# Sum steps fewer ahead of the first norm, low parts behind the copies of dilated keys, a head's four squares together

## The chip, the cores and the metric

The kernel runs on one core of a Trainium2 chip, in one launch. The time is the device time in microseconds (us). A core has five engines, each with an instruction stream of its own that it takes in order: TensorE (PE in the profile) multiplies matrices, VectorE (DVE), ScalarE (ACT) and GpSimd (POOL) work on tiles, and SyncE (SP) here only issues transfers. Engines wait for each other by semaphores. DMA transfers are put into queues by SP and POOL (in the profile SPq and POOLq are those engines' issuing) and are carried out by 16 DMA engines that all queues share.

## The reference

One layer of a decoder trunk, in float32, for 512 tokens of 1024 channels:

```python
proj = x @ w_in                               # 1024 -> 10752
o_da = diff_attention(...)                    # 4 heads: two softmax maps, w = p0 - lam * p1
                                              # o * rsqrt(mean(o^2) + eps) * norm_g, per head
o_sb = stick_breaking_attention(...)          # 8 heads
o_dl = dilated_attention(...)                 # 12 heads in 3 groups, dilations 1, 4, 16
merged = g0 * (o_da @ w_da) + g1 * (o_sb @ w_sb) + g2 * (o_dl @ w_dl)    # g = sigmoid(gates)
x = layer_norm(ALPHA * x + merged @ w_out)    # the first norm
c = square(relu(x @ w_up)) @ w_down           # 1024 -> 4096 -> 1024
ple = sigmoid(x @ w_ple_gate) * (p @ w_ple)
x = layer_norm(ALPHA * x + c + ple)
```

The inputs are x, p and the weights; the output is x. The first norm's result is the input of both the MLP and the gate of `ple`.

## The kernel before

**Products.** A float32 product is three PE matmuls on high and low parts (`mm3`, L86 to L89: high x high, low x high, high x low). Most of the large products are in a form with seven instead of eight block products, which needs sums of weight blocks. These sums are made in DRAM, by transfers from DRAM to DRAM on POOL's queue: a copy, then transfers that add to it. `vsum`, `qsum`, `msum`, `bsum`, `gsum`, `usum` and `dsum` are such sums, `usum` those for w_up and `dsum` those for w_down; names like `usum_3` in the order below are buffers of them. Each such transfer is a *sum step* (`sum_steps`; issued at L1247 when it adds, at L1249 when it copies), and it waits for a mark, the DVE subtraction that made the low part of a weight chunk some four chunks earlier.

**Weights.** A weight chunk (128x1024) is loaded by SP (L213, some by POOL at L176) into one of six raw buffers `raw`. ACT casts it to its high part `wh` (L262), DVE subtracts for the low part `wl` (L264), into a ring of five; PE reads both. A load into a raw buffer goes out when the subtraction has freed the buffer.

**The order.** The main loop goes through a list of *items*, each some matmuls with a bank of PSUM and an evacuation, and between them takes pieces of the heads' work (generators, `step`). Behind each item it adds to `credit`: the item's size times its `rate` up to the fifth item of the output product, nothing for a stretch, and 0.72 an item from the seventh behind the start of `ple`. Each whole credit issues one sum step. So `rate` says how many sum steps an item brings. From this program a scheduler makes each engine's order; `tc.high_priority()` lets an instruction come early in it, and `tc.issue_after(i)` puts what is inside behind instruction `i`.

**The three places.**

- *Dilated keys.* The projection's product for a dilated head's keys `dl_k` is computed into a PSUM bank and copied out by DVE at high priority (L346, in `t_evac`). `u4l` and `u5l` (L292) are low parts of sums of x that the seven-product form needs; their high parts `u4h` and `u5h` are cast on ACT (L291). `oT` (L1885) and `e`, `sph`, `spl`, `sml` (L1820 to L1857) are stick-breaking attention's.
- *Differential heads.* `da_block` handles one head and one block of 128 queries: logits, exponentials (L1916), transposes of the weights, the product with the values (L1944) into a quarter of a bank `po` that the head's four blocks share, and a square on ACT with its sum over the row (L1949, tile `scr`, sums in `ss`). After the fourth block come mean and root (L1954 to L1963, tile `ms`), the product of `po` with them (L1965, tile `on`), transposes on PE (L1971) and a copy to `oT`.
- *First norm.* `wout_items` computes merged @ w_out in eight items (four blocks of 128 tokens, two halves of 512 channels), each with rate 3.2 (L1055). Behind a block's second half `layer_norm_act` runs: sums of squares on ACT, two steps of the variance on DVE (L1001, L1002, tile `lr`), the power -1/2 on POOL (L1003), then the scaled rows `xn` on DVE (L1005, L1013). PE transposes `xn` (L1078), ACT casts it to `x1hT` (L1084) and DVE makes the low part `x1lT` (L1085); ACT makes `x1r` (L1091). The product `p @ w_ple` (L1109 to L1111) lies beside this; the gate product (L1169 to L1171) reads the norm's result, and the up products come after it, copied out by ACT (L1358, tile `up`).

Of the kernel before, what the change touches and what calls it, by code (L numbers as in the profile page):

```python
# [10 lines left out]
F32 = mybir.dt.float32  # L11
F32R = mybir.dt.float32r
BF16 = mybir.dt.bfloat16
AF = mybir.ActivationFunctionType
# [4 lines left out]
P = 128  # L19
# [36 lines left out]
def trunk(tc, a, out):  # L56
    nc = tc.nc
    es = ExitStack()
    with es:
        big = es.enter_context(tc.tile_pool(name="big", bufs=64))  # L60
        ring = es.enter_context(tc.tile_pool(name="ring", bufs=1))
        one = es.enter_context(tc.tile_pool(name="one", bufs=1))
# [7 lines left out]
        def nm(s):  # L70
            uid[0] += 1
            return f"{s}_{uid[0]}"

        def slot(name, dt=F32):
            return big.tile([P, 512], dt, name=nm(name), tag="s", bufs=NSLOT)
# [79 lines left out]
        st = {"dma": 0, "split": 0, "ring": 0}  # L155
# [12 lines left out]
        def chunk(src, w):  # L168
            return chunk_of(load(src, w))
# [68 lines left out]
        def split_next():  # L238
            c = chunks[st["split"]]
            w, off = c["w"], c.get("off", 0)  # L240
            if c.get("pre"):
                c["pre"]()
            st["ring"] += not c.get("aside")
            if c.get("apart"):
                hs, ls = [[slot(n, F32R) for _ in range(2)] for n in ("wh", "wl")]
                parts = [(hs[i], ls[i], 512 * i, 512 * i + 512) for i in range(2)]
                c["h"], c["l"] = Halves(hs), Halves(ls)
            elif c.get("beside"):
                h, lo = c["beside"]["tiles"]
                parts = [(h[:, 512:512 + w], lo[:, 512:512 + w], 0, w)]  # L250
                c["h"], c["l"] = parts[0][:2]
            elif c.get("dst") is None:
                h = ring.tile([P, 1024], F32R, name=nm("wh"), tag="wh", bufs=RING)
                lo = ring.tile([P, 1024], F32R, name=nm("wl"), tag="wl", bufs=RING)
                parts = [(h[:, :w], lo[:, :w], 0, w)]
                c["h"], c["l"] = parts[0][:2]
                c["tiles"] = h, lo
            else:
                parts = c["dst"]
            for h, lo, a0, a1 in parts:  # L260
                raw = c["from"]["raw"][:, off + a0:off + a1]
                i = nc.scalar.copy(h, raw)  # L262
                st["cast"] = getattr(i, "ins", i)
                i = nc.vector.tensor_sub(lo, raw, h.bitcast(F32))  # L264
                st["low"] = getattr(i, "ins", i)
                lows.append(st["low"])
                marks.append(st["low"])
            for t in (c["from"], *c.get("also", ())):
                t["uses"] -= 1
            if c.get("then"):  # L270
                c["then"]()
            st["split"] += 1
# [11 lines left out]
        items = []  # L284
# [24 lines left out]
        scale = {"da_q": 0.125, "sb_q": 0.125, "dl_q": 128.0 ** -0.5}  # L309
# [18 lines left out]
        def t_evac(name, j):  # L328
            def ev(ps):
                sc = scale.get(name, 1.0)  # L330
                if name in ("sb_k", "da_q"):
                    T[name, j] = evac_stacked(ps, name, sc)
                elif name in ("sb_q", "da_k"):
                    T[name, j] = evac_twice(ps, name, sc)
                else:
                    t = slot(name)
                    if j < 4:
                        o, i = t, ps
                    else:
                        o = t.rearrange("p (c n) -> p c n", c=4)  # L340
                        i = ps.rearrange("p (n c) -> p c n", c=4)
                    if name == "dl_q":
                        nc.scalar.activation(o, i, AF.Copy, scale=sc)
                    else:
                        with tc.high_priority():
                            nc.vector.tensor_copy(o, i)  # L346
                    T[name, j] = t
            return ev

# [678 lines left out]
        def wout_items():  # L1028
            for half in range(2):
                cs = [chunk(a["wo"][half, c].rearrange("p k n -> p (k n)"), 1024) for c in range(4)]  # L1030
                for tt in range(4):
                    ks = (4, 5, 6, 7, 0, 1, 2, 3) if tt == 2 and not half else range(8)

                    def mm(ps, tt=tt, cs=cs, ks=ks):
                        for k in ks:
                            c = cs[k // 2]
                            s = slice((k % 2) * 512, (k % 2) * 512 + 512)
                            h, lo = merged_T[k // 4, tt // 2, k % 4 // 2]
                            q = slice(k % 2 * 256 + tt % 2 * P, k % 2 * 256 + tt % 2 * P + P)
                            nc.tensor.matmul(ps, h[:, q], c["h"][:, s], start=k == ks[0], stop=False)  # L1040
                            nc.tensor.matmul(ps, h[:, q], c["l"][:, s], start=False, stop=False)
                            nc.tensor.matmul(ps, lo[:, q], c["h"][:, s], start=False, stop=k == ks[-1])

                    def ev(ps, tt=tt, half=half):
                        y = xn.pop((tt, half))
                        if not half:
                            x1sum[tt] = small("lsm", 2)
                        i = nc.vector.scalar_tensor_tensor(y, y, ALPHA, ps, op0=OP.mult, op1=OP.add,
                                                           accum_out=x1sum[tt][:, half:half + 1])
                        st["added"] = getattr(i, "ins", i)  # L1050
                        x1[tt, half] = y
                        if half:
                            pending.append(ln1_gen(tt))
                    item(cs if tt == 3 else [], mm, ev, need=cs, bank=at_bank)
                    items[-1]["rate"] = 3.2  # L1055
                    for t in {0: [(1, 1, 0), (1, 1, 1)], 1: [(0, 1, 0), (0, 1, 1)]}.get(tt, ()) if not half else ():
                        turn_item(*t)

# [834 lines left out]
        da_ss = {}  # L1893
        da_rr = {}
        da_left = {}

        def da_block(hd, qb):
# [7 lines left out]
            for m in range(2):  # L1905
# [5 lines left out]
                                               scale=1.0, scalar=-3.0e38, op0=OP.add, op1=OP.max,  # L1911
                                               accum_out=mx[:, m:m + 1])
# [7 lines left out]
            r = da_rr[hd][:, qb:qb + 1]  # L1920
# [20 lines left out]
            po = da_po[hd]  # L1941
            qs = slice(qb * P, qb * P + P)
            for kb in range(qb + 1):
                nc.tensor.matmul(po[:, qs], wT[:, kb * P:kb * P + P], V["da_v", 0, kb][:, hd * P:hd * P + P],  # L1944
                                 start=kb == 0, stop=kb == qb, skip_group_check=True)
            scr = one.tile([P, P], F32, name=nm("scr"), tag="scr", bufs=2)
            ss = da_ss[hd]
            with tc.high_priority():
                nc.scalar.activation(scr, po[:, qs], AF.Square, scale=r, accum_out=ss[:, qb:qb + 1])  # L1949
            da_left[hd] -= 1  # L1950
            if da_left[hd] == 0:
                yield

                nc.vector.tensor_scalar(ss, ss, 1.0 / P, EPS, op0=OP.mult, op1=OP.add)  # L1954
                y = small("ir", 4)
                nc.scalar.activation(y, ss, AF.Ln)
                e = nc.scalar.activation(y, y, AF.Exp, scale=-0.5)
                last_exp[0] = getattr(e, "ins", e)
                yield
                nc.vector.scalar_tensor_tensor(ss, ss, -0.5, y, op0=OP.mult, op1=OP.mult)  # L1960
                nc.vector.tensor_mul(ss, ss, y)
                nc.vector.scalar_tensor_tensor(ss, ss, 1.5, y, op0=OP.add, op1=OP.mult)
                nc.vector.tensor_mul(ss, ss, da_rr[hd])  # L1963
                on = slot("on")
                nc.vector.tensor_mul(on.rearrange("p (b d) -> p b d", b=4), po.rearrange("p (b d) -> p b d", b=4),  # L1965
                                     ss.unsqueeze(2).to_broadcast([P, 4, P]))
                yield
                yield
                tp = at_bank()
                for b in range(4):  # L1970
                    nc.tensor.transpose(tp[:, b * P:b * P + P], on[:, b * P:b * P + P], ident)  # L1971
                oT[hd] = slot("oT")
                nc.scalar.activation(oT[hd], tp, AF.Copy, scale=gcol)
                ready.add(hd)
# [198 lines left out]
        credit = 0.0  # L2173
# [3 lines left out]
        for n, it in enumerate(items):  # L2177
# [44 lines left out]
            if 5 <= n < wout_at + 5:  # L2222
                credit += it["size"] * it.get("rate", 1.0)
            elif n > ple_at + 6:
                credit += 0.72
            while credit >= 1:
                credit -= 1
                next(sum_steps_, None)
# [148 lines left out]
```

## Time and profile before

| | |
|---|---|
| median of 3 runs | 1033.77 us (1033.19 to 1034.73) |
| profiled execution | 1031.9 us, span 1030.2 us |
| mean granted TensorE clock in it | 0.997 |
| PE busy | 1016.4 us (99%) |
| DVE, ACT, POOL busy | 796.5, 614.7, 208.5 us |
| DMA | 275.99 MB, mean 268 GB/s |

The span reaches from the first to the last instruction; the execution's time has 1.7 us around it. A busy engine is one that has an instruction under way; PE at a lower clock is busy too, for longer. The *granted clock* is the share of full speed that PE was given. In a row such as "160.57 1.23 DVE L264 TENSOR_TENSOR wl<-raw,wh ... [0.97 <-ACT wh L262]" the numbers are the start and the length in us, L264 is the code line, `wl` is written from `raw` and `wh`, and the bracket says that the engine had stood idle for 0.97 us until ACT's instruction that writes `wh` ended.

### The profile page before, as it was taken

To read this page: it belongs to the slowest core of one execution; us is meant where nothing else is said; L and a number is where in the kernel's file an instruction comes from. 1 tells how busy PE (TensorE), PEld (TensorE's weight loads), DVE (VectorE), ACT (ScalarE), POOL (GpSimd) and SP (SyncE) were. 2 spreads that over 40 slices of the span, in tenths; PEclk is the share of its full clock that TensorE was granted. 3 is DMA by queue.
4 is the path that set the end of the run, shared out by engine and by line. 5 is a ranking of instruction groups with operands and counts; after the bars stand their busy time and mean duration, and the time that the engine had idled before them with its cause. 6 is when DMAs were issued, how large, how long until landed. Compare 5 with 4: busy or idle time off the path is not lost.

```text
span 1030.2 us, 15635 instructions
## 1 busy us (share of the span) xinstructions
PE 1016.4 (99%) x5626; PEld 880.8 (86%) x5626; DVE 796.5 (77%) x1411; ACT 614.7 (60%) x1055; POOL 208.5 (20%) x311
## 2 busy tenths in 40 slices
PE   9999999999999999999999999899999999999997
PEld 7888887788998898888888888789999899899886
DVE  6888697788657777787788876697768777777975
ACT  7566566775544656556655733776666556556651
POOL 0322320121412224111221140221121212111101
PEclk9999999999999999999999999999999999999999
DMA  8999993888899999989999994789999999999922
GB/s 311 282 308 287 254 269 103 208 209 266 275 322 276 274 279 273 286 222 299 284 270 299 305 306 162 171 236 333 322 322 345 301 347 306 328 313 292 310 79 82
DMA packets 79885, 275.99 MB, mean 268 GB/s; under 512 B 9816, under 2 KB 10600, under 8 KB 79808
## 3 DMA queue, kind: packets, MB, share of 16 engines
q0 software_dynamic: 37712, 135.08, 52.1%
q1 hardware_dynamic: 41520, 138.99, 36.8%
q8 instruction: 44, 0.72, 0.3%
q10 hardware_dynamic: 576, 0.92, 0.2%
q14 instruction: 33, 0.27, 0.1%
HBM read 267.59 MB, written 116.42 MB: 373 GB/s over the span
## 4 chain that ended last, share of the span: by engine, by line
PE 88%; DVE 3%; DMA 3%; issue 2%; ACT 2%; POOL 1%; DVEq 0%; POOLq 0%; ACTq 0%
PE mm L87 9%; PE mm L88 9%; PE mm L89 9%; PE at L1430 4%; PE at L1431 4%; PE at L1432 4%; PE at L750 2%; PE at L752 2%; PE at L751 2%; PE at L89 2%; PE at L88 2%; PE at L87 2%; PE mm L750 2%; PE mm L752 2%; PE mm L751 2%
## 5 line engine op out<-in xcount | busy, mean ns | idle before, releaser
L264 DVE TENSOR_TENSOR wl<-raw,wh 128x1024 fp32r<-128x1024 f32 (+1 forms) x274 | 330.3, 1214 | 105.0 <-ACT wh L262 103.7
L262 ACT CAST wh<-raw 128x1024 fp32r<-128x1024 f32 (+1 forms) x274 | 284.4, 1043 | 206.0 <-PE mm L88 104.3
L87 PE MATMUL mm<-xhT,wh 128*128 128x512 f32 (+1 forms) x254 | 95.5, 376 | 1.1 <-DVE dl_k L346 1.1
L89 PE MATMUL mm<-xhT,wl 128*128 128x512 f32 (+1 forms) x254 | 94.3, 371 | 0.0
L88 PE MATMUL mm<-xlT,wh 128*128 128x512 f32 (+1 forms) x254 | 94.1, 370 | 0.0
L1430 PE MATMUL at<-wh,hh 128*128 128x512 f32 x188 | 73.7, 392 | 0.0
L1431 PE MATMUL at<-wl,hh 128*128 128x512 f32 x188 | 73.7, 392 | 0.0
L1432 PE MATMUL at<-wh,hl 128*128 128x512 f32 x188 | 73.1, 389 | 0.0
L87 PE MATMUL mm<-x1hT,wh 128*128 128x256 f32 x256 | 72.8, 284 | 0.3 <-ACT up L1358 0.3
L89 PE MATMUL mm<-x1hT,wl 128*128 128x256 f32 x256 | 72.4, 283 | 0.0
L88 PE MATMUL mm<-x1lT,wh 128*128 128x256 f32 x256 | 72.4, 283 | 0.0
L87 PEld LDWEIGHTS mm<-xhT,wh 128*128 128x128 f32 x254 | 47.9, 189 | 8.9 <-issue 1.2
L89 PEld LDWEIGHTS mm<-xhT,wl 128*128 128x128 f32 x254 | 47.8, 188 | 8.2
L88 PEld LDWEIGHTS mm<-xlT,wh 128*128 128x128 f32 x254 | 47.9, 189 | 7.5
L1247 POOL DMA_DIRECT2D usum<-in_wu_dram x32 | 27.5, 861 | 120.8 <-DVE wl L264 43.9
L87 PEld LDWEIGHTS mm<-x1hT,wh 128*128 128x128 f32 x256 | 48.9, 191 | 2.3 <-ACT up L1358 0.5
L88 PEld LDWEIGHTS mm<-x1lT,wh 128*128 128x128 f32 x256 | 48.9, 191 | 1.5
L89 PEld LDWEIGHTS mm<-x1hT,wl 128*128 128x128 f32 x256 | 48.9, 191 | 0.0
L1247 POOL DMA_DIRECT2D dsum<-in_wd_dram x28 | 23.1, 824 | 120.4 <-DMA dsum<-dsum 32.4
L1432 PEld LDWEIGHTS at<-wh,hl 128*128 128x128 f32 x188 | 35.3, 188 | 7.6
L1430 PEld LDWEIGHTS at<-wh,hh 128*128 128x128 f32 x188 | 35.5, 189 | 6.2
L1431 PEld LDWEIGHTS at<-wl,hh 128*128 128x128 f32 x188 | 35.5, 189 | 5.7
(676 smaller groups left out, 2859.8 us busy)
## 6 DMA issues: line engine op xcount, KB each, us to landing
usum<-in_wu_dram POOLq DMA_DIRECT2D x48, 512.0 KB, 10.1
dsum<-in_wd_dram POOLq DMA_DIRECT2D x42, 512.0 KB, 9.1
raw<-usum SPq DMA_DIRECT2D x32, 512.0 KB, 9.1
raw<-dsum SPq DMA_DIRECT2D x28, 512.0 KB, 7.7
raw<-in_wt_dram SPq DMA_DIRECT2D x26, 512.0 KB, 7.2
raw<-in_wd_dram SPq DMA_DIRECT2D x25, 512.0 KB, 9.0
raw<-in_wu_dram SPq DMA_DIRECT2D x24, 512.0 KB, 8.8
qsum<-in_wq_dram POOLq DMA_DIRECT2D x18, 512.0 KB, 9.1
```

The lines of the kernel that those rows point to most:

```text
L87: nc.tensor.matmul(ps, wh, xh, start=start, stop=False, skip_group_check=True)
L88: nc.tensor.matmul(ps, wh, xl, start=False, stop=False, skip_group_check=True)
L89: nc.tensor.matmul(ps, wl, xh, start=False, stop=stop, skip_group_check=True)
L262: i = nc.scalar.copy(h, raw)
L264: i = nc.vector.tensor_sub(lo, raw, h.bitcast(F32))
L750: nc.tensor.matmul(ps, h[:, q], c["h"][:, n], start=go, stop=False, skip_group_check=True)
L751: nc.tensor.matmul(ps, h[:, q], c["l"][:, n], start=False, stop=False, skip_group_check=True)
L752: nc.tensor.matmul(ps, lo[:, q], c["h"][:, n], start=False, stop=end, skip_group_check=True)
L1247: i = nc.gpsimd.dma_start(o, i, accum_op=OP.add, max_dma_last_dim=4096)
L1430: nc.tensor.matmul(ps, h[:, q], c["h"][:, s], start=go, stop=False, skip_group_check=True)
L1431: nc.tensor.matmul(ps, h[:, q], c["l"][:, s], start=False, stop=False, skip_group_check=True)
L1432: nc.tensor.matmul(ps, lo[:, q], c["h"][:, s], start=False, stop=end, skip_group_check=True)
```

## The change

1. `split_next` puts the next low part that is written after a dilated key's copy behind this copy in the order. The copy stores itself in `st["evac"]`, and the next low part takes it out.
2. `da_block` no longer squares after each block. After the fourth block the four squares of the head run one behind the other. The squares read `po` in quarters as before.
3. The rate of the output product's items is 2.4 instead of 3.2. Behind the start of `ple` an item brings 0.75 instead of 0.72 credits.

```diff
@@ split_next
                 st["cast"] = getattr(i, "ins", i)
-                i = nc.vector.tensor_sub(lo, raw, h.bitcast(F32))
+                with ExitStack() as behind:
+                    if "evac" in st:
+                        behind.enter_context(tc.issue_after(st.pop("evac")))
+                    i = nc.vector.tensor_sub(lo, raw, h.bitcast(F32))
@@ t_evac
                         with tc.high_priority():
-                            nc.vector.tensor_copy(o, i)
+                            ins = nc.vector.tensor_copy(o, i)
+                        st["evac"] = getattr(ins, "ins", ins)
@@ wout_items
-                    items[-1]["rate"] = 3.2
+                    items[-1]["rate"] = 2.4
@@ da_block
-            scr = one.tile([P, P], F32, name=nm("scr"), tag="scr", bufs=2)
-            ss = da_ss[hd]
-            with tc.high_priority():
-                nc.scalar.activation(scr, po[:, qs], AF.Square, scale=r, accum_out=ss[:, qb:qb + 1])
             da_left[hd] -= 1
             if da_left[hd] == 0:
+                ss = da_ss[hd]
+                with tc.high_priority():
+                    for b in range(4):
+                        scr = one.tile([P, P], F32, name=nm("scr"), tag="scr", bufs=2)
+                        nc.scalar.activation(scr, po[:, b * P:b * P + P], AF.Square, scale=da_rr[hd][:, b:b + 1],
+                                             accum_out=ss[:, b:b + 1])
                 yield
@@ main loop
             elif n > ple_at + 6:
-                credit += 0.72
+                credit += 0.75
```

How it moves instructions. On DVE, around the first copy of a dilated key, before (a row is: line, operation, output<-inputs, shape):

```order
L1846 TENSOR_TENSOR sml_1725<-e_1714,smh_1724 128x384
L292 TENSOR_TENSOR u4l_1731<-xr_1697,u4h_1730 128x512
L264 TENSOR_TENSOR wl_1814<-raw_1372,wh_1813 128x1024
L292 TENSOR_TENSOR u4l_1735<-xr_1699,u4h_1734 128x512
L346 COPY dl_k_1754<-mm_1701 128x512
L1885 TENSOR_TENSOR oT_1767<-at_1758,ot_1768 64x512
L292 TENSOR_TENSOR u5l_1772<-xr_1477,u5h_1771 128x512
```

And after, at the same place on DVE:

```order
L1850 TENSOR_TENSOR sml_1725<-e_1714,smh_1724 128x384
L295 TENSOR_TENSOR u4l_1731<-xr_1697,u4h_1730 128x512
L295 TENSOR_TENSOR u4l_1735<-xr_1699,u4h_1734 128x512
L349 COPY dl_k_1754<-mm_1701 128x512
L1889 TENSOR_TENSOR oT_1767<-at_1758,ot_1768 64x512
L295 TENSOR_TENSOR u5l_1772<-xr_1477,u5h_1771 128x512
L267 TENSOR_TENSOR wl_1814<-raw_1372,wh_1813 128x1024
```

The low part `wl_1814` has moved from two places ahead of the copy to three places behind it. On PE the first matmul that reads it stands about 60 rows behind the matmul that reuses the copied bank.

On ACT, the squares of the first differential head, before:

```order
L1949 ACTIVATE scr_3900,ms_3898<-at_3897,rr_3675 128x128
L262 CAST wh_3852<-raw_3449 128x1024
L1949 ACTIVATE scr_3904,ms_3898<-at_3897,rr_3675 128x128
L262 CAST wh_3889<-raw_3455 128x1024
L96 COPY wT_3910<-at_3906 128x384
```

And after, at the end of the head's fourth block on ACT:

```order
L262 CAST wh_4029<-raw_3717 128x1024
L1956 ACTIVATE scr_4041,ms_3898<-at_3897,rr_3675 128x128
L1956 ACTIVATE scr_4043,ms_3898<-at_3897,rr_3675 128x128
L1956 ACTIVATE scr_4045,ms_3898<-at_3897,rr_3675 128x128
L1956 ACTIVATE scr_4047,ms_3898<-at_3897,rr_3675 128x128
L1962 ACTIVATE ir_4096<-ms_3898 128x4
```

The first two squares have left their places between casts and stand with the other two ahead of the root (`ir`).

On POOL, around the four powers of the first norm (`lr`), before:

```order
L1249 DMA usum_3_134<-usum_1_132 128x1024
L1003 TENSOR_TENSOR lr_6589<-lr_6589,mhalf 128x1
L1003 TENSOR_TENSOR lr_6629<-lr_6629,mhalf 128x1
L176 DMA raw_6367<-in_wg_dram 128x1024
L1003 TENSOR_TENSOR lr_6693<-lr_6693,mhalf 128x1
L1247 DMA dsum_1_156<-in_wd_dram 128x1024
L176 DMA raw_6527<-in_wg_dram 128x1024
L1247 DMA usum_3_134<-in_wu_dram 128x1024
L1249 DMA dsum_3_158<-dsum_1_156 128x1024
L1003 TENSOR_TENSOR lr_6739<-lr_6739,mhalf 128x1
L1247 DMA dsum_3_158<-in_wd_dram 128x1024
```

And after, on POOL:

```order
L1007 TENSOR_TENSOR lr_6588<-lr_6588,mhalf 128x1
L1007 TENSOR_TENSOR lr_6628<-lr_6628,mhalf 128x1
L176 DMA raw_6367<-in_wg_dram 128x1024
L1007 TENSOR_TENSOR lr_6692<-lr_6692,mhalf 128x1
L1253 DMA usum_3_134<-usum_1_132 128x1024
L176 DMA raw_6526<-in_wg_dram 128x1024
L1251 DMA dsum_1_156<-in_wd_dram 128x1024
L1007 TENSOR_TENSOR lr_6738<-lr_6738,mhalf 128x1
L1251 DMA usum_3_134<-in_wu_dram 128x1024
L1253 DMA dsum_3_158<-dsum_1_156 128x1024
L1251 DMA dsum_3_158<-in_wd_dram 128x1024
```

The copy of `usum_3` has moved from ahead of the first power to behind the third, and the add to `usum_3` and the copy of `dsum_3` from ahead of the fourth power to behind it.

## The prediction

> **What bounds the kernel.** I read the head of the page first, to see which engine carries the span, and then the list of what TensorE waited for.
>
> ```profile
> span 1030.2 us, 15635 instructions
> PE 1016.4 (99%) x5626; PEld 880.8 (86%) x5626; DVE 796.5 (77%) x1411; ACT 614.7 (60%) x1055; POOL 208.5 (20%) x311
> ```
> PE is busy for 1016.4 of 1030.2 us. An edit that leaves the matmuls alone, as this one does, can only win back PE's waits (and stretches at a lower clock, which count as busy), or add to them. PE's waits, by the line that waited and the line it waited for (us in total, times, longest):
>
> ```profile
> PE at L1169 <- ACT x1r L1091: 1.7, 1, 1.7
> PE at L1627 <- DVE zero L1624: 1.2, 1, 1.2
> PE at L1078 <- DVE xn L1013: 1.1, 1, 1.1
> PE mm L87 <- DVE dl_k L346: 1.1, 1, 1.1
> PE at L1944 <- ACT scr L1949: 0.7, 1, 0.7
> PE at L1852 <- ACT sph L1826: 0.5, 1, 0.5
> PE mm L87 <- ACT up L1358: 0.3, 1, 0.3
> ```
> Rows 1 and 3 belong to the first norm, row 4 to the dilated keys, row 5 to the squares of the differential heads. These four, 4.6 us together, are what the change can reach directly. The zeroing in row 2 lies at the start and isn't touched. Row 6 (stick-breaking) and row 7 (the copy of an up product) lie behind two of the places that change, so a gain may be given back there.
>
> **The dilated keys.** Timeline rows (start, length, engine, line, output<-input; in brackets the idle time before and who ended it) of the place where row 4 arises:
>
> ```profile
> 160.44 0.62 ACT L291 CAST u4h<-xr 128x512 fp32r<-128x512 f32 x1
> 160.57 1.23 DVE L264 TENSOR_TENSOR wl<-raw,wh 128x1024 fp32r<-128x1024 f32 x1 [0.97 <-ACT wh L262]
> 161.71 0.69 DVE L292 TENSOR_TENSOR u4l<-xr,u4h 128x512 fp32r<-128x512 f32 x1
> 162.31 0.68 DVE L346 COPY dl_k<-mm 128x512 f32<-128x512 f32 x1
> 163.14 0.47 PE L87 MATMUL mm<-xhT,wh 128*128 128x512 f32 x1 [1.06 <-DVE dl_k L346]
> ```
> DVE takes its work in order. It stood idle until the cast, ran the low part `wl` at 160.57, then `u4l`, then the `dl_k` copy, and PE came back at 163.14, 0.83 us after that copy began: the matmul's bank is free only when the copy is done. With the low part behind the copy, `u4l` is next. Its input `u4h` on ACT begins at 160.44 and lasts 0.62, so `u4l` can start at 161.06 at the earliest, instead of 161.71. The copy keeps its distance to `u4l` (0.60) and starts at 161.66 instead of 162.31. PE gains 0.65 us of its 1.1. The price is a low part that comes some 3 us later, behind `u5l` in the new order. The matmuls that read it stand about 60 rows behind the stalled one in PE's order; PE takes 1016.4 / 5626 = 0.18 us a row on the mean, so some 11 us cover the delay and I cost it at nothing. Without that cover the whole 0.65 would go. Next on that path is the wait on `sph` (row 6, 0.5 us): low parts change places with stick-breaking work there too, and it may swallow the gain or vanish with it. I take 0.6, with 0 and 1.1 (all of row 4) as ends.
>
> **The squares.** Around the wait on `scr`, and the end of the first head's chain:
>
> ```profile
> 356.69 0.71 ACT L1916 ACTIVATE lg<-lg,mx 128x512 f32<-128x512 f32 x1
> 357.39 0.35 ACT L1949 ACTIVATE scr<-at,rr 128x128 f32<-128x128 f32 x1
> 357.89 0.71 PE L1944 MATMUL at<-dl_v,wT 128*128 128x128 f32 x4 [0.72 <-ACT scr L1949]
> 375.72 0.69 DVE L1965 TENSOR_TENSOR on<-at,ms 128x512 f32<-128x512 f32 x1
> 381.68 0.60 PE L1971 MATMUL at<-ident,on 128*128 128x128 f32 x4
> ```
> The square of a block stood on ACT behind an exponential (356.69 + 0.71) and ran at 357.39; the next block's matmuls write into the same bank and waited for it until 357.89. Without a square after each block nothing reads that bank between the blocks, and row 5 goes: 0.7 us. It is the only one of the 16 squares that PE waited for. The four squares of a head are the same instructions, now together: three more of 0.36 stand ahead of the head's mean, 1.1 us on ACT. Behind the mean come the product (375.72 + 0.69 = 376.41) and the transposes on PE at 381.68: the 5.3 us between them cover the 1.1. Were that cover gone, the transposes would be up to 1.1 us late in each of four heads. ACT's work queued behind the four squares is late by the same 1.1; that no square but one had anyone wait for it is why I cost this at nothing. I take 0.7, with 0.3 and 0.9 as ends (half of it turning up elsewhere; the wait in PE's pitch instead of its idle time).
>
> **The first norm.** The output product ends in four norms of 128 tokens. Each takes a power on POOL (`lr`, L1003) between two parts on DVE. The last of the four:
>
> ```profile
> 659.59 0.56 POOL L1249 DMA_DIRECT2D dsum<-dsum  x1 [4.96 <-DMA dsum<-in_wd_dram]
> 660.16 0.58 POOL L1003 TENSOR_TENSOR lr<-lr,mhalf 128x1 f32<-128x1 f32 x1
> 657.29 0.14 DVE L1002 TENSOR_SCALAR lr<-lr 128x1 f32<-128x1 f32 x1
> 660.78 1.41 DVE L1013 SCALAR_TENSOR_TENSOR xn<-xn,lr,ln_b 128x512 f32<-128x512 f32 x2 [3.34 <-POOL lr L1003]
> 663.25 0.68 DVE L1085 TENSOR_TENSOR x1lT<-at,x1hT 128x512 fp32r<-128x512 f32 x1
> 663.96 0.65 ACT L1091 COPY x1r<-at 128x256 f32<-128x256 f32 x2 [3.31 <-DVE x1lT L1085]
> 661.68 1.29 PE L1078 MATMUL at<-ident,xn 128*128 128x128 f32 x8 [1.08 <-DVE xn L1013]
> 664.66 0.50 PE L1169 MATMUL at<-wh,x1hT 128*128 128x512 f32 x1 [1.70 <-ACT x1r L1091]
> ```
> DVE had the power's input ready at 657.29 + 0.14 = 657.43. The power ran at 660.16, because on POOL it stands behind the issue of a copy `dsum<-dsum` (659.59, after 4.96 us of waiting) that must wait until the sum it copies from has landed. Everything after hangs on that power: `xn` at 660.78, PE's transposes at 661.68, the split `x1lT` at 663.25, ACT's `x1r` at 663.96, PE's gate product at 664.66. In the new order that copy stands behind the fourth power, since the lower rate of the items before leaves the stream of sums a step or two behind; ahead of the power are issues of transfers that wait for no landing there. So it can start at 657.45 rather than 660.16, and the chain comes 2.7 us earlier. PE waited for this chain twice (rows 3 and 1: 1.1 and 1.7), so the 2.7 lie on its path wholly, and the gate product starts at about 662.0.
>
> There is more to gain there than the waits. Two neighbouring stretches (length, PE's busy time and count, granted clock, DMA share, GB/s):
>
> ```profile
> 661.97:665.38 3.41, 1.68 (x11) 1.00 1.05 291
> 665.38:668.80 3.42, 3.42 (x10) 0.50 0.58 224
> ```
> To 665.38 PE was busy for 1.68 us of 3.41, and in the next stretch it ran at half clock: 3.42 us for work of 1.7. Without the gap ahead of it I expect this to go too. On PE the two make 2.7 + 1.7 = 4.4 us by 669.
>
> The Trainium skill, "TensorE: Matmul & The Clock Gate", Part 1 (What's actually happening), says that the clock falls after an idle window of about 3.4 us, in windows that run freely; the slow stretch of 3.42 us agrees with that length. No single wait here is longer than 1.7 us, and by that rule alone the clock would not have fallen and the norm would save 2.7 and no more on PE; Part 4 (PE-mode transpose) of the page says that transposes don't count as busy in the same way, which joins the two waits around the eight transposes into one gap of some 4 us and fits the trace.
>
> How much of the 4.4 survives? The next thing that PE waits for is row 7, so I looked at what feeds it: stretches of DVE (length, busy time, clock, DMA share, GB/s), a piece of the chain that ends there, and the rows at the wait.
>
> ```profile
> 664.00:672.00 8.00, 4.54 (x7) 0.79 0.73 234
> 672.00:680.00 8.00, 8.00 (x12) 1.00 0.90 215
> 690.00:700.00 10.00, 9.77 (x14) 1.00 1.05 331
> 700.00:708.00 8.00, 8.00 (x11) 1.00 1.04 324
> 695.22 12.58 DMA raw<-usum
> 707.90 1.05 ACT L262 CAST wh<-raw 128x1024 fp32r<-128x1024 f32 x1 [1.35 <-DMA raw<-usum]
> 709.27 0.39 PE L87 MATMUL mm<-x1hT,wh 128*128 128x256 f32 x1 [0.30 <-ACT up L1358]
> ```
> From 672 on DVE is full (8.00 of 8, 9.77 of 10, 8.00 of 8) and PE runs ahead of it. A load of an up sum goes out at 695.22, after a low part on DVE has freed its buffer, and takes 12.58 us. ACT's cast at 707.90 waits for it, the copy `up` stands behind the cast on ACT, and PE behind that copy, 0.3 us. So if PE arrives 4.4 us earlier, it keeps only what the landing gains. DVE gets its `xn` 2.7 us sooner and has some 0.3 us of idle time to lose up to 700, so the load goes out about 3.0 us earlier; with as much transfer work ahead of it as before, it lands 3.0 earlier, and PE's wait there grows from 0.3 to 0.3 + 4.4 - 3.0 = 1.7. Hence I take 3.0 for this part. The upper end is 4.7 (4.4 and the old wait), if the landing isn't what holds.
>
> For the lower end: POOL's sums share the DMA engines with that load, whose mean share is 1.05 and 1.04, so a sum more ahead of it delays it by what a sum takes. The row of POOL's queue (packets, MB, share of 16 engines) prices one:
>
> ```profile
> q0 software_dynamic: 37712, 135.08, 52.1%
> ```
> The first and the last sum issued ahead of the load:
>
> ```profile
> 682.38 0.87 POOL L1249 DMA_DIRECT2D dsum<-in_wd_dram  x1
> ...
> 691.37 0.82 POOL L1247 DMA_DIRECT2D dsum<-in_wd_dram  x1 [1.10 <-DMA dsum<-in_wd_dram]
> ```
> At 512 KB (0.524 MB) each, 135.08 MB are 258 transfers, and 52.1% of 1030.2 us over 258 is 2.1 us each. From 682.38 to 691.37 five sums were issued, three copies and two adds. Sums there wait for a low part's mark or for the landing ahead of them, both of which move with DVE, so I count five after too, one add replaced by a copy. One more would take 2.1 of the 3.0; that gives the lower end, 0.9.
>
> The Trainium skill, "DMA: Bandwidth & Descriptors", Queues, rings and completion order, says that each DMA engine takes turns between its queues packet by packet. By that rule a postponed sum takes engine time from a load issued earlier as well, which speaks against the change and is the rival of more sums below; no row here shows single packets taking turns.
>
> The rate of 0.75 for 0.72 acts behind the norm, where most steps wait for the landing before them. I cost it at nothing, with 0.5 to either side, a quarter of a sum's 2.1.
>
> **Sum.** 0.6 + 0.7 + 3.0 = 4.3 us. The profiled execution took 1031.9 (span 1030.2 and 1.7 around it) and would take 1027.6. The median of the runs is 1033.77, 1.87 above it; I subtract the same from the median: 1029.5. This kernel's measurement can tell about 0.2%, 2.1 us, from no change.
>
> **Rivals.**
> The landing moves with PE in full: the norm gives 4.7, all together 6.0: 1027.8. For it: DVE was idle for 3.5 us of 664 to 672, while PE ran slow. Against it: DVE is full afterwards.
>
> The clock falls again, where the wait has grown to 1.7: 1.7 more, gain 2.6, 1031.2. For it: the drop at 665 followed waits no longer than 1.7. Against it: there were two of them, and the wait of 1.1 at 163.14 stands alone like this one.
>
> One sum more ahead of the load: the norm gives 0.9, all together 2.2, 1031.6. Two more, -1.2 and 0.1 in all, 1033.7. Or the fourth power still waits, so that the change doesn't do what it says: 1.3, 1032.5. Against the last stands the power's place in the new order. I take the latter two as "no change".
>
> Slower: the postponed steps bunch, four of them ahead of the load. It then lands 4 x 2.1 - 3.0 = 5.4 us later than now and PE waits on `up` until it does; with the 1.3 of the first two parts 4.1 are lost: 1037.9. It decides from a landing 3.4 us later than 707.8 (3.4 - 1.3 = 2.1). For it: the DMA share of 1.05. Against it: the rate postpones one or two steps.
>
> **Numbers.** Likeliest, 0.46: 1029.5 (its own range 1028 to 1031). Landing in full 0.15, clock 0.11, one sum 0.10, no change 0.12, slower 0.06. Faster, below 1031.7, takes the first three and half of the fourth, 0.77; same 0.17; slower 0.06. The range from 1026.6 (the first rival, and 1.2 for the upper ends of the first two parts and the rate) to 1032.5 leaves out the slower rival and half of no change.
>
> **What the profile after would show.** In the list of PE's waits no row with `scr` and none with `xn`; `dl_k` at about 0.5, `x1r` below 0.7. POOL's fourth `lr` right behind DVE's, with no wait for a landing. No half clock around 665. At the copy `up`, a wait of 1 to 2 us where there was 0.3: that is the step I am least sure of. The forecast is wrong if the load behind that copy lands no earlier than 707.8, if a wait of like size turns up behind `sph` or in the gate product, or if the fourth power still follows the copy of a sum.

## The result and the profile after

| | before | changed |
|---|---|---|
| median of 8 runs | 1032.39 us | 1028.32 us |
| ratio to before | | 0.9961 (0.9947 to 0.9974) |
| profiled execution, span | 1030.2 us | 1026.4 us |
| mean granted TensorE clock in it | 0.997 | 0.999 |

The change makes the kernel 4.0 us shorter (2.7 to 5.5 by the interval). The forecast was 4.3 shorter. Ratios and their intervals are worked out from all the runs, so a ratio need not equal the quotient of the medians beside it. One of the changed kernel's eight runs took 2613.1 us and is left out of the ratio (the median of the other seven is 1028.16). That forecast and result agree doesn't yet say that the steps do, so here is first the list of PE's waits in the changed kernel (total, times, longest):

```profile
PE at L1631 <- DVE zero L1628: 1.2, 1, 1.2
PE at L567 <- DVE dl_v L580: 0.9, 1, 0.9
PE at L1856 <- ACT sph L1830: 0.9, 1, 0.9
PE mm L87 <- ACT up L1383: 0.7, 1, 0.7
PE at L1173 <- ACT x1r L1095: 0.5, 1, 0.5
PE mm L87 <- DVE dl_k L349: 0.4, 1, 0.4
PE at L500 <- ACT wh L262: 0.3, 1, 0.3
```
Against the list of before: `scr` and `xn` are gone, `x1r` has fallen from 1.7 to 0.5, and `dl_k` from 1.1 to 0.4. `sph` has grown from 0.5 to 0.9, `up` from 0.3 to 0.7, and `dl_v` is new with 0.9. By this list the gain lies in the norm and the squares, and part 1 has given back more than it won. (The wait of 0.3 at L500 lies in the first 12 us, in which the executions differ by up to 1.2 us whatever the kernel; the changed one came out of them 0.5 us ahead of the one before.)

The first norm, timeline rows of POOL, DVE and PE, and two stretches of PE (length, busy time, granted clock, DMA share, GB/s):

```profile
657.57 0.56 POOL L1007 TENSOR_TENSOR lr<-lr,mhalf 128x1 f32<-128x1 f32 x1 [3.17 <-DVE lr L1006]
664.52 0.55 POOL L1253 DMA_DIRECT2D dsum<-dsum  x1 [2.66 <-DMA dsum<-in_wd_dram]
658.17 1.41 DVE L1017 SCALAR_TENSOR_TENSOR xn<-xn,lr,ln_b 128x512 f32<-128x512 f32 x2 [0.68 <-POOL lr L1007]
662.06 0.50 PE L1173 MATMUL at<-wh,x1hT 128*128 128x512 f32 x1 [0.53 <-ACT x1r L1095]
659.90:663.30 3.40, 2.87 (x17) 1.00 1.02 281
663.30:666.70 3.40, 3.40 (x16) 1.00 1.03 272
```
The fourth power runs at 657.57 and no longer behind a copy of a sum, which now goes out at 664.52. `xn` starts at 658.17 where it was 660.78, and the gate product at 662.06 where it was 664.66: 2.6 us, against 2.7 forecast. No stretch there runs at half clock.

The place where the gain was to be cut, a stretch of DVE and then rows of ACT and PE:

```profile
664.00:672.00 8.00, 7.56 (x10) 1.00 0.86 258
703.27 1.05 ACT L262 CAST wh<-raw 128x1024 fp32r<-128x1024 f32 x1 [0.95 <-PE mm L88]
712.87 1.05 ACT L262 CAST wh<-raw 128x1024 fp32r<-128x1024 f32 x1 [0.98 <-DMA raw<-in_wu_dram]
714.24 0.39 PE L87 MATMUL mm<-x1hT,wh 128*128 128x256 f32 x1 [0.71 <-ACT up L1383]
```
DVE is busy for 7.56 of the 8 us from 664 to 672, where it was 4.54 before. The cast that waited for a load until 707.90 now starts at 703.27, 4.6 us earlier, and isn't held by a transfer (PE's last read of the ring slot released it). A later load holds instead: the cast at 712.87 waits for it and PE for 0.7 us at 714.24.

The dilated keys, the copy and PE behind it, then ACT and PE some 35 us later:

```profile
161.20 0.68 DVE L349 COPY dl_k<-mm 128x512 f32<-128x512 f32 x1
161.94 0.50 PE L87 MATMUL mm<-xhT,wh 128*128 128x512 f32 x1 [0.36 <-DVE dl_k L349]
196.69 0.60 ACT L1824 ACTIVATE e<-at 128x512 f32<-128x512 f32 x1 [1.51 <-DMA values<-dl_v]
203.47 0.50 PE L567 MATMUL at<-wh,u4h 128*128 128x512 f32 x1 [0.89 <-DVE dl_v L580]
```
The copy starts at 161.20 and PE's wait is 0.36 us instead of 1.06, 0.7 less, as worked out. But at 196.69 ACT has waited 1.51 us for a transfer of values to land, and PE pays for that at 203.47.

### The profile page after: what moved, and what is told of

Read it like the earlier page. It is cut to its first block, busy times and chain, and to the rows that moved or that the text cites. A ratio compares the mean times of both kernels' runs of the same rounds, so it can differ in the third digit from the quotient of the medians.

```text
span 1026.4 us, 15627 instructions
## 1 busy us (share of the span) xinstructions
PE 1014.2 (99%) x5626; PEld 878.8 (86%) x5626; DVE 796.0 (78%) x1411; ACT 613.6 (60%) x1055; POOL 208.1 (20%) x311
## 4 chain that ended last, share of the span: by engine, by line
PE 82%; issue 7%; DVE 6%; DMA 2%; ACT 2%; POOL 1%; DVEq 0%; POOLq 0%; ACTq 0%
PE mm L87 9%; PE mm L89 8%; PE mm L88 8%; PE at L1434 4%; PE at L1435 4%; PE at L1436 4%; DVE wl L267 2%; PE at L754 2%; PE at L756 2%; PE at L755 2%; PE at L89 2%; PE at L88 2%; PE at L87 2%; PE mm L756 2%; PE mm L754 2%
```

## The experiments

**Each part alone.** The first is part 1 on the kernel before:

```diff
-                i = nc.vector.tensor_sub(lo, raw, h.bitcast(F32))
+                with ExitStack() as behind:
+                    if "evac" in st:
+                        behind.enter_context(tc.issue_after(st.pop("evac")))
+                    i = nc.vector.tensor_sub(lo, raw, h.bitcast(F32))
...
+                        st["evac"] = getattr(ins, "ins", ins)
```

> Part 1 alone (low parts behind the copies of dilated keys). Theory A, the order that part 1 leaves behind costs more than it wins: PE's wait on dl_k falls from 1.1 to about 0.4, but the wait on sph is 0.9 instead of 0.5 and a wait on dl_v of 0.9 near 202 is there as well, since both come from the order; all together 0.7 us slower than before (0.0 to 1.0). Theory B, the wait on dl_v was one slow landing of a transfer of values in one execution: the row with dl_v is absent or below 0.2, and the time is 0.3 to 0.6 us shorter than before.

Measured: 1032.54 us against 1031.89, ratio 1.0008 (0.9999 to 1.0017). Three of its rows of PE's waits:

```profile
PE at L567 <- DVE dl_v L580: 2.3, 1, 2.3
PE at L1856 <- ACT sph L1830: 0.9, 1, 0.9
PE mm L87 <- DVE dl_k L349: 0.4, 1, 0.4
```
Theory A holds in kind: the wait on `dl_k` fell as forecast, `sph` and `dl_v` came. In time the interval just reaches "no change". The wait on `dl_v` is even 2.3 us in this execution, which is the longest of the eleven (1034.69 us). The rows that lead to it, the issue of the second transfer of values on POOL and the ACT instruction that waits for its landing:

```profile
190.00 0.56 POOL L524 DMA_DIRECT2D values<-dl_v  x1 [0.94 <-DVE dl_v L577]
198.36 0.60 ACT L1824 ACTIVATE e<-at 128x512 f32<-128x512 f32 x1 [3.01 <-DMA values<-dl_v]
```
Issued at 190.00, and ACT goes on at 198.36; in the changed kernel the same transfer was issued at 189.83 and ACT went on at 196.69. Before, ACT started the same instruction at 195.87 without idle time; the cast ahead of it had waited 0.30 us for this transfer. The transfer's time from issue to landing was 5.0 us before and 6.8 and 8.3 us in these two executions. In all, it was 4.8 to 6.0 us in the nine profiled executions without part 1 and 6.8 to 8.3 in the five with it.

The squares alone:

```diff
-                nc.scalar.activation(scr, po[:, qs], AF.Square, scale=r, accum_out=ss[:, qb:qb + 1])
...
+                    for b in range(4):
```

> Part 2 alone (the four squares of a head together). Theory A, the parts add: the wait on scr goes and nothing takes its place, 0.7 to 0.9 us shorter than before. Theory B, ACT's work behind four squares in a row gives it back: a new row of 0.3 us or more after 369 in PE's waits, and less than 0.4 us shorter.

Measured: ratio 0.9991 (0.9983 to 1.0), 0.9 us at its middle. Its whole list of PE's waits:

```profile
PE at L1169 <- ACT x1r L1091: 1.7, 1, 1.7
PE at L1627 <- DVE zero L1624: 1.2, 1, 1.2
PE mm L87 <- DVE dl_k L346: 1.1, 1, 1.1
PE at L1078 <- DVE xn L1013: 1.0, 1, 1.0
PE at L1852 <- ACT sph L1826: 0.5, 1, 0.5
PE mm L87 <- ACT up L1358: 0.2, 1, 0.2
```
`scr` is gone and no new row is there: theory A, by this list. But the list has no waits under 0.15 us, and small ones have come inside one row: eight transposes near 419 (`at<-ident,L`) take 1.35 to 1.39 us in eight of the nine profiled executions with the new squares and 1.03 to 1.06 in all five with the old ones. In the ninth, the kernel with part 1 and 0.72 below, the row falls in two and the list names the wait: `PE at L2102 <- DVE on L1971: 0.2`. That is the product `on` of the second head, behind its squares and its mean. Followed by the starts of the same matmuls, PE wins 1.0 us at 358 (0.7 of it the wait) and gives some 0.35 back near 419.

The lower rate alone:

```diff
-                    items[-1]["rate"] = 3.2
+                    items[-1]["rate"] = 2.4
```

> Rate 2.4 alone. Theory A, nearly all of the change is the first norm, and DVE's idle time while PE ran at half clock is won as well, so that the loads move with PE: 3.6 to 4.2 us shorter, no stretch below full clock, the wait on up at 0.5 to 0.9 as in the changed kernel. Theory B, the landing of a load of up sums keeps 1.4 us back, as I had forecast: 3.0 us shorter (2.6 to 3.3) and a wait on up of 1.4 to 1.9.

Measured: 1027.42 us against 1031.89, ratio 0.9952 (0.9938 to 0.9965): 5.0 us by the ratio (3.6 to 6.4), 4.5 by the medians. In the middle that is more than the whole change, but the intervals overlap. PE's waits:

```profile
PE at L1627 <- DVE zero L1624: 1.2, 1, 1.2
PE mm L87 <- DVE dl_k L346: 1.1, 1, 1.1
PE at L1944 <- ACT scr L1949: 0.7, 1, 0.7
PE at L1169 <- ACT x1r L1091: 0.5, 1, 0.5
PE at L1852 <- ACT sph L1826: 0.5, 1, 0.5
```
And DVE in the stretch behind the norm:

```profile
664.00:672.00 8.00, 7.56 (x11) 1.00 0.67 175
```
Not even the old wait on `up` is left, and DVE has 7.56 us of work in those 8 as in the changed kernel. Theory B, my step, falls: no wait on `up` of 1.4 us or more holds anything back. Theory A is right in kind; it had left a wait of 0.5 to 0.9 on `up`, and its 3.6 to 4.2 us lie within the interval, below the middle. What the half clock adds varies; the section on the clock comes to that.

**The change without part 1**, with the 0.75 (the diff is part 1 undone).

> The changed kernel without part 1. Theory A, part 1 costs: 0.3 to 1.0 us shorter than the changed kernel, that is 4.5 to 5.0 shorter than before; PE's list has dl_k at 1.1 and sph at 0.5 again and no dl_v. Theory B, part 1 gains: 0.3 to 0.6 longer than the changed kernel, some 3.6 shorter than before.

Measured: 1027.81 us against 1031.89, ratio 0.9956 (0.9944 to 0.9969), and waits on `dl_k` of 1.1, `sph` 0.5, `up` 0.7, none on `dl_v`. That is 0.5 us less than the changed kernel's median, but the intervals overlap; by itself this run doesn't settle it.

**The same change with 0.72**, with part 1.

```diff
-                credit += 0.75
+                credit += 0.72
```

> The changed kernel with 0.72 in place of 0.75 (part 1, the squares, rate 2.4). Theory A, part 1 costs 0.7 us by its later waits on sph and dl_v: 0.5 to 1.0 longer than the kernel without part 1, with dl_v in the list of PE's waits. Theory B, part 1 is neutral: within 0.3 of it.

Measured: 1026.88 us against 1032.37, ratio 0.9956 (0.9944 to 0.9969); waits on `dl_v` 1.1, `sph` 0.9, `dl_k` 0.4, and no row for `up`. The kernel that differs from it by part 1 alone is the next one, 1027.15 us beside it on the same chip: in time that is theory B, part 1 is neutral. By its waits part 1 costs as in theory A, and the wait on `up` is gone. Five runs each, from 1026.3 to 1029.2 and from 1026.5 to 1028.1, don't tell the two apart.

**Squares and 2.4 alone**, with 0.72 and without part 1.

> Parts that gained alone, together: the four squares and the rate 2.4, with 0.72 kept and without part 1. Theory A, the parts add and 0.75 costs what the wait on up (0.7) shows in the kernels that have it: 5.3 to 5.8 us shorter than before, the wait on up near 710 gone, and 0.7 us or more shorter than the changed kernel without part 1. Theory B, 0.75 is neutral and the wait on up a matter of how early PE arrives: a wait on up of 0.5 or more here too, and 4.3 to 4.8 shorter than before.

Measured: 1027.15 us against 1032.37, ratio 0.9954 (0.994 to 0.9968), no wait on `up`: theory A by the wait. Its 5.3 to 5.8 us are not shown: 4.7 by the ratio (3.3 to 6.2), 5.2 by the medians. A second run beside the changed kernel on one chip:

> The changed kernel once more, beside the kernel without part 1 and 0.75. Theory A (part 1 costs some 0.5, 0.75 some 0.5): 0.7 to 1.5 us longer than that one, with waits on dl_v, sph and up in its list. Theory B (both neutral): within 0.4 of it.

> The four squares and rate 2.4 alone, once more, beside the changed kernel on one chip. Theory A: 0.7 to 1.5 us shorter than the changed kernel, 5 us shorter than before, no waits on dl_v and up of over 0.3. Theory B: the same as the changed kernel within 0.4.

Measured: 1026.64 us for the two parts alone, ratio 0.9949 (0.9937 to 0.9961), against 1028.36, ratio 0.9969 (0.9957 to 0.9981), for the changed kernel: 1.7 us apart, six runs of one (1027.34 to 1030.13) all above the five of the other (1026.09 to 1026.9). The list of the two parts alone:

```profile
PE at L1627 <- DVE zero L1624: 1.2, 1, 1.2
PE mm L87 <- DVE dl_k L346: 1.1, 1, 1.1
PE at L1169 <- ACT x1r L1091: 0.5, 1, 0.5
PE at L1852 <- ACT sph L1826: 0.4, 1, 0.4
PE at L496 <- ACT wh L262: 0.2, 1, 0.2
```
The changed kernel had a wait on `dl_v` of 1.7 in this execution, `sph` 0.9, and `up` 0.2. So this smaller change beats both kernels. The pair differs by part 1 and by 0.75 together, and no pair of runs divides the 1.7 us between them. The profiled executions divide it, as far as they are typical of the runs, when the same matmul is followed through each of them and that of the kernel before. Part 1: the lead of 0.7 us that PE has from the copy at 163 is gone again by 191 in all five executions with it, and from 195 to 210, at the wait on `dl_v`, PE loses 1.2, 1.9, 1.4, 2.0 and (with a stretch at half clock) 4.0 us; in eight other executions without part 1 it loses 0 to 0.8 there. The 0.75: from 655 to 760 PE gains 4.6 to 4.7 us in the five executions with rate 2.4 and 0.72, and 3.8, 3.8 and 4.4 in the three with 0.75, whose wait on `up` is 0.7, 0.7 and 0.2 (no row for `up` in the five).

**What makes the values late.** Part 1, squares and 2.4, with one sum step held back: the add to `qsum` that POOL issues at 191, behind the second transfer of values, goes out behind two loads.

```diff
-            while credit >= 1:
+            while credit >= 1 and not (st.get("sums", 0) == 45 and st.setdefault("held", 5) > 0):
                 credit -= 1
                 next(sum_steps_, None)
+                st["sums"] = st.get("sums", 0) + 1
+            if st.get("sums", 0) == 45 and credit >= 1:
+                st["held"] -= 1
```

> The same as the kernel with part 1, the squares and rate 2.4, but one sum step (an add to qsum, issued at 191 just behind two transfers of values) goes out some items later, behind two loads; no other engine's order differs. Theory A, that the wait on dl_v comes from the second transfer of values, which shares the DMA engines with this add and so lands late: it lands within 5.5 us of its issue, the wait on dl_v is below 0.3, and the time is 0.6 to 1.2 us shorter than with the add in its old place. Theory B, it is the weight loads, which the new order puts later, that it shares with: it lands 6.5 us or more after its issue as before, and the wait on dl_v stays at 0.9 or more.

Measured: 1029.7 us against 1032.37, ratio 0.9976 (0.9967 to 0.9985), 2.8 us longer by the medians than without the hold. POOL's issue, ACT's wait for the landing, and two rows of PE's waits:

```profile
189.97 0.56 POOL L524 DMA_DIRECT2D values<-dl_v  x1 [0.94 <-DVE dl_v L577]
197.67 0.60 ACT L1824 ACTIVATE e<-at 128x512 f32<-128x512 f32 x1 [2.34 <-DMA values<-dl_v]
PE at L1880 <- ACT ah L1870: 1.8, 1, 1.8
PE at L567 <- DVE dl_v L580: 1.7, 1, 1.7
```
The values still land late (issued 189.97, ACT released for 197.67), so it isn't this add: theory A falls. The add that was held met a later transfer of values instead: ACT's `ah` waits 2.4 us for it at 227 and PE 1.8. What is left is theory B, that the loads are the other party. Two rows speak for it, the stretch from 184 to 188 before and then after (length, clock, DMA share, GB/s):

```profile
184.00:188.00 4.00, 1.00 0.70 115
```
And of the changed kernel:

```profile
184.00:188.00 4.00, 1.00 0.49 84
```
The DMA engines were busy for 0.70 of these 4 us before and for 0.49 in the changed kernel, though PE was 0.2 to 0.5 us further on there. A load that POOL issued at 185.32 goes out at 185.84 in the changed kernel, behind a DVE row that changed places, so 0.8 us of the engines' time fall empty, and I take it that the queue that the values join is longer for it. This share is 0.70 to 0.92 in the nine executions without part 1 and 0.30 to 0.56 in the five with it. Within the two groups, though, it doesn't go with the landing: the kernel before has the lowest share of the nine and one of the fastest landings. So theory B is argued from rows and not shown; a kernel that moves only those loads wasn't tried.

**The clock.** The kernel before with four matmuls added ahead of the norm's last eight transposes and seven behind them, their results thrown away:

```diff
+                if tt == 3 and not h:
+                    for _ in range(4):
+                        nc.tensor.matmul(tp, pTs[0][0][:, 0:P], pTs[0][0], start=True, stop=True, ...)
```

> The kernel before with eleven matmuls added on PE whose results are thrown away: four just ahead of the eight transposes of the first norm, seven behind them, on operands that are ready, so that PE is busy in the gap while the fourth power stays late. Theory A, the half clock after 665 comes from the gap alone: no stretch below full clock there, the gate product starts at about the same time as before (664.7, within 0.5), and PE stands 1.5 to 1.8 us earlier at 670. Theory B, the clock falls for another reason: 3.4 us at half clock in spite of the filling, and no gain. The final time may gain less than 1.7, since the rows of DVE behind the norm come in another order here.

Measured: 1032.21 us, ratio 1.0005 (0.9996 to 1.0013). Rows of PE, and the stretch where the half clock stood:

```profile
660.95 1.07 PE L1079 MATMUL at<-pTh 128*128 128x512 f32 x4
661.88 1.38 PE L1081 MATMUL at<-ident,xn 128*128 128x128 f32 x8
664.95 1.89 PE L1169 MATMUL at<-pTh 128*128 128x512 f32 x7 [1.69 <-ACT x1r L1094]
665.00:668.40 3.40, 3.40 (x15) 1.00 0.79 307
```
The clock stays at full in this execution. But the seven didn't fill the wait: the scheduler gave them the bank that `x1r` is read from, they start after it at 664.95, and the gate product starts about 1.7 us later behind them. Those 1.7 us and the 1.7 of the clock cancel in this execution. And the other runs don't all agree with it: five of the eleven have a mean granted clock of 0.996 and take 1033.3 to 1034.0 us, six have 0.998 or 0.999 and take 1031.8 to 1032.2. A stretch of 3.41 us at half clock takes 3.41 x 0.5 / 1030 = 0.0017 off the mean, so one or more of them very likely came back in those five; no profile shows where. So the second test has the first four only:

> The kernel before with four matmuls added on PE ahead of the first norm's last eight transposes, their results thrown away, on operands that are ready: they fill only idle time of PE, and the fourth power stays late. Theory A, the clock falls when a window of about 3.4 us that lies anywhere falls into the gap from 660.4 to 664.7, so that before it cost none, one or two windows of 1.7 us, as in three kernels with the same gap: with the gap cut to less than 3.4 us no execution falls to half clock there, the median is 1 to 2 us shorter than before and the runs lie within 2 us (before: 3.6 us). Theory B, the gap's length has no part in it: half clock after 665 in the profile, and the spread and the time of before.

Measured: 1030.48 us against 1031.56, ratio 0.999 (0.9982 to 0.9999), 1.1 us shorter, nine of its eleven runs between 1029.87 and 1031.07. Its profiled execution shows no half clock at 665, though a granted clock of 0.95 up to 737, which I can't explain: its matmuls behind the gap start every 0.23 us, as at full clock. Of the other ten runs nine record 0.998 or 0.999 and one 0.997. Both tests speak for the gap as the cause. Cutting it by the length of four matmuls was enough in most runs of the second test; in five of the first, which has the same four there, it very likely wasn't, and I can't say why.

How much the gap costs is another matter. In part 1 alone, with the same two waits in the norm, stretches of PE (length, busy time and count, clock, DMA share, GB/s):

```profile
664.02:668.30 4.28, 1.65 (x11) 1.00 1.04 266
668.30:671.70 3.40, 3.40 (x15) 1.00 0.79 308
202.24:205.65 3.41, 1.10 (x5) 1.00 0.70 227
205.65:209.06 3.41, 3.41 (x9) 0.50 0.20 80
666.45:669.86 3.41, 1.72 (x9) 1.00 1.05 318
```
And of the squares alone:

```profile
662.85:669.67 6.82, 5.83 (x14) 0.50 0.77 263
```
One execution of the same gap ran on at full clock, one (the kernel before) had one window of 3.42 us at half, one had two, 6.82 us. A wait of 2.3 us on `dl_v`, without transposes, brought a window at half clock at 205.65 by itself. So taking the gap away is worth 0, 1.7 or up to 3.4 us in an execution, on top of the waits; this fits the wide range of the kernel before (1030.17 to 1034.09 in 21 runs) beside that of rate 2.4 alone (1026.77 to 1027.47 in 5). The clocks on record say the same: of 60 runs of the kernel before, the 19 at 0.998 or above take 1031.4 us on the mean, the 31 at 0.997 take 1032.2 and the 10 below 1033.0, and none of the 26 runs with a lower rate and without part 1 is below 0.998.

The Trainium skill, "TensorE: Matmul & The Clock Gate", Part 1 (What's actually happening), has the window in which PE's activity is watched run freely, and these runs agree: the same gap falls otherwise into the windows each time. In the stretch of 3.41 us just ahead of each drop PE was busy for 1.68 us (before), 1.66 (squares) and 1.10 (part 1, at 202); counted on in such steps from the drop at 205.65, the two windows that share the norm's gap in part 1 have 2.5 and 1.72 us (666.45 above), and the clock stays. Its table "Why this matters for your kernels" warns of gaps above some 3 us; here 2.3 us were enough once.

**Fewer sums still.** Squares, rate 1.6 and 0.72:

```diff
-                    items[-1]["rate"] = 2.4
+                    items[-1]["rate"] = 1.6
```

> The four squares and rate 1.6 instead of 2.4, with 0.72: one or two sum steps fewer ahead of the first norm again. Theory A, 2.4 has already taken from the fourth power all that stood ahead of it, and the sums have room: within 0.5 us of the kernel with 2.4. Theory B, postponed sums get ahead of loads in the stretch of 690 to 720, each 2.1 us of the DMA engines: a wait on up of 1 us or more near 710, and 0.8 to 2 us longer than with 2.4.

Measured: 1026.29 us, ratio 0.9949 (0.9936 to 0.9962): the same as 2.4 by the median (1026.64 on this chip), theory A. But two of its six runs took 1028.3 and 1028.7, four 1025.8 to 1026.5, and one of the long ones has its profile:

```profile
PE at L1431 <- DVE wl L264: 1.0, 1, 1.0
```
This wait lies at 974. ACT's cast at 959.93 had waited 5.52 us for a load of a sum for w_down, and the last step of the sums goes out at 962.93 there, against 955.13 with rate 2.4. So in this execution steps put off at 650 seem to be paid for 320 us later, and not at 700 as theory B had it; that the other long run has the same wait isn't shown.

## Why the prediction was right, and where it wasn't

The time was right: 4.3 us forecast, 4.0 measured. Two steps were wrong, with opposite signs, and that they nearly cancel is luck: part 1 came out about 1.4 us worse than forecast and part 3 some 1.7 to 2.0 better by itself. One of the prediction's own signs of being wrong, a wait of 1 to 2 us behind `sph`, came close: waits of 0.9 us on `sph` and on `dl_v` stand behind the dilated keys.

*The dilated keys: wrong sign.* Forecast 0.6 shorter, measured alone 0.8 longer (0.1 shorter to 1.8 longer). That the sign is wrong rests on the traces; the interval still holds zero, and the pair with rate 2.4 and 0.72 shows no difference. The local step was right to 0.05 us. What failed is the wait on `sph`, of which the prediction said "it may swallow the gain or vanish with it" and which I then left out of the value, and the assumption that nothing else hangs on the new order. Scheduling the copy earlier moved stick-breaking matmuls up on PE and, behind them, casts, low parts and loads. The waits on `sph` (0.4 more) and `dl_v` (0.9 to 2.3) are there in all five executions with part 1 and in none of the nine without; which of the moved rows makes the values late stays open.

*The squares: right in the main.* Forecast 0.7, measured 0.9 (0 to 1.8). The wait on `scr` went. But the 1.1 us that now stand ahead of the mean are not wholly hidden, as the prediction had it from the first head: at the second head `on` comes later and PE's transposes near 419 pay some 0.35 us. Followed along PE's rows the part nets about 0.6.

*The first norm: right mechanism, one term too small.* The power moved by 2.6 us (2.7 forecast), and the half clock went (1.7 forecast, as in the profiled execution; elsewhere none or twice that). The term that was mis-sized is what survives at the copy `up`: I let the loads gain 3.0 us because DVE "has some 0.3 us of idle time to lose". The row from 664 to 672 that I had quoted for a rival showed 3.5 us of idle time right in front of that. DVE won 3.0 of them (4.54 to 7.56), and the cast behind the load moved by 4.6 us; the wait on `up` is 0.7 where 1 to 2 were forecast. The rival "the landing moves with PE in full" was the right one: its 4.7 is what PE gains at the norm in the profiled execution of rate 2.4 alone, whose runs gained 5.0 (3.6 to 6.4) where I had put 3.0. The rival that the clock falls again is in no profile of the changed kernel, though one of its seven runs (1031.13 us) has a mean clock of 0.996. The price of 2.1 us for a sum, which went only into the lower ends, is a mean of all that POOL's queue carries; 208 of POOL's 290 issues are sums, and no run shows the price of one by itself.

*The rate 0.75: forecast at nothing with 0.5 to either side.* The wait on `up` of 0.7, 0.7 and 0.2 goes with it. That it costs 0.3 to 0.8 us is read from the traces; no pair of runs separates it in time.

*Sums in the way of loads: not seen at 700* with 2.4 or 1.6; at 1.6 late sums show at 974.

So the gain of part 3 was larger than forecast, and part 1 took a part of it back. In the two profiled executions the sum comes out: PE is 0.5 us ahead from the start, which is chance, loses 1.2 by part 1, gains 0.6 by the squares and 4.7 at the norm, and gives 0.8 back at `up`: 3.8, the difference of the spans.

## What to carry to other kernels

An engine that looks full behind a stall may have been idle just ahead of it, because the stall itself starved it: before you let such an engine limit a gain, take the idle time in the stretch that begins with the stall. An edit that wins one local wait by moving an instruction has to be followed in the new order of every engine up to the next waits, loads and stores included; here a wait of 1.1 us became 0.4, and the 0.7 won were gone 28 us later, with a new wait behind them. And where a change has several parts, run them alone: the version without part 1 and 0.75 is 1.7 us faster than the change.

## What was unexpected of the hardware

The same gap on PE (some 4.2 us with eight transposes in it) was followed by none, one or two stretches of 3.4 us at half clock in three executions, and a single wait of 2.3 us by one. A transfer of 256 KB took 4.8 to 6.0 us in nine executions without part 1 and 6.8 to 8.3 us in the five with it, although the transfers around it are the same and only some were issued half a microsecond later.
